# RWKV bonus sums and head layernorm of a hybrid diffusion step: products with constant matrices in two fp32r parts instead of one fp32 product

## The chip, the cores and the metric

The kernel runs on one core of one Trainium2 chip. Its time is the device time of one execution in microseconds (us); of a kernel the median of its runs counts. Five engines work beside each other, each through its own list of instructions in order: TensorE (PE, with PEld for its weight loads), VectorE (DVE), ScalarE (ACT), GpSimd (POOL) and SyncE (SP), which issues most of the transfers. TensorE writes into banks of PSUM, from which ACT or DVE take results.

## The reference, cut to what matters

Two layers of a diffusion trunk over 128 context and 256 latent tokens (T = 384 columns side by side), width 1024. The first layer's mixer holds a Mamba-2 group and an RWKV-7 group; the second holds GLA and mLSTM. The change touches the last lines of the RWKV group (16 heads of 64 channels):

```python
def head_layernorm(x, w, b, n_heads):
    xf = x.reshape(shp[:-1] + (n_heads, shp[-1] // n_heads)).astype(jnp.float32)
    mu = jnp.mean(xf, axis=-1, keepdims=True)
    var = jnp.mean(jnp.square(xf - mu), axis=-1, keepdims=True)
    y = ((xf - mu) * lax.rsqrt(var + RWKV_LN_EPS)).reshape(shp).astype(x.dtype)
    return y * w + b
...
y_rw = head_layernorm((ys_rw[0] + ys_rw[1]).reshape(bsz, t, D_RWKV), p['rwkv_ln_w'], p['rwkv_ln_b'], RWKV_HEADS)
bonus = jnp.sum(rh * kh * p['rwkv_r_k'], axis=-1, keepdims=True) * vh
y_rw = (y_rw + bonus.reshape(bsz, t, D_RWKV)) * g
out = jnp.concatenate([y_ssd, y_rw], axis=-1) @ p['w_out']
```

## The kernel before

Channels lie on the 128 partitions and tokens along the free axis, so an RWKV tile j (0 to 7) is two heads by 384 tokens. A mean or a sum over the 64 channels of a head is then a product with a constant 128x128 matrix: `blk` (ones within a head) gives a head's sum on each of its partitions, and `cen` (identity less 1/64 within a head) takes the mean away. Three such products are made for each j, 24 in all, each one fp32 matmul of 128x384:

- in `rw_bonus` (line 1169): `pb = blk @ rk`, with rk = r * r_k * k in a tile whose name is `t` in the trace; then `bo = v * pb` on DVE;
- in `rw_tail` (line 1451): `pm = cen @ y`; ACT squares it into a tile `t` and copies it back to y; then a second product `blk @ sq`, which the trace also calls `pm<-t`; ACT makes 1/sqrt from it (Ln, Exp), DVE multiplies, adds the bonus and multiplies with the gate product `pg`.

A fourth product of this kind, `pn` (the norm of kk in `rw_shared`), is not touched. The large products (`dps`, projections and MLP) are already made in parts: weights and activations are split in a high part of type fp32r (an ACT copy, line 277) and a low part (a DVE subtraction, line 235), and a product is three fp32r matmuls, high by high, high by low and low by high.

The mixer of the first layer fills the stretch from about 60 to 860 us. `ab_streams` (line 1527) goes through 19 rounds. In a round several generators run interleaved: `tail` (j of two rounds ago), `chain` (the recurrence), `inv` (inverses of 64x64 triangles in f16), `prep` with the bonus at its end, `ssd` (Mamba), and `fill` (dense projections, the modulation product `mod`, at the end the output projection). `run` (line 1584) calls the generator that is furthest behind, and a table of paces weights them. The instructions are so written in one sequence; when the program is built, each engine's list is then put in an order by estimates of when operands and buffers are ready, so that what is written side by side can stand apart. On the chip each engine keeps to its list: an instruction that waits holds up all behind it.

Buffers that matter here: `psP` has two PSUM banks, shared in turn by `pb`, `pm`, `pn`, `pw`, `pa`, `pst`, `pg` and the pairs of `psc`. The pool `misc` has the tags `nh` (two buffers: the neighbour sums `nb` of the token shift) and `nt` (two buffers: the gate temporaries `sg`, and `yr`, the tiles of the mixer's output that `reload` (line 1904) brings back from HBM). In round 16 `ab_norm` (line 1855) reloads eight such tiles through the two `nt` buffers, scales each on DVE and splits it (`sH` on ACT, `sL` on DVE) for the output projection. In round 18 the tail of j = 7 ends the mixer; its y is split and multiplied with `wlast` in `ab_out_last` (line 1937), with the modulation products `mod` of the second layer in between.

Of the kernel before, what the change touches and what calls it, by code (L numbers as in the profile page):

```python
# [8 lines left out]
F32 = mybir.dt.float32  # L9
F32R = mybir.dt.float32r  # L10
# [4 lines left out]
ALU = mybir.AluOpType  # L15
# [6 lines left out]
T = 384  # L22
# [153 lines left out]
class Net:  # L176
# [903 lines left out]
    def rw_evac(self, idx, make, act=True):  # L1080
# [14 lines left out]
            self.stt(out[:, 128:T], nb[:, 129:385], self.mu_h[:, idx:idx + 1], out[:, 128:T], ALU.mult, ALU.add)  # L1095
        return evac

    def rw_low(self):

        self.sigmoid(self.wdt, self.wdt, scale=2.0)  # L1100
        self.ts(self.wdt, self.wdt, 2.0, ALU.mult, -1.0, ALU.add)
# [67 lines left out]
    def rw_bonus(self, j, sh):  # L1169
        rk = self.rpp.tile([128, T], F32, tag="t1", name="t1", bufs=1)  # L1170
        self.stt(rk, sh["r"], self.par("rwkv_r_k", j), sh["k"], ALU.mult, ALU.mult)
        yield
        pb = self.psp("pb")
        self.mm(pb[:, :T], self.c("blk"), rk)
        sh["bo"] = bo = self.rpc.tile([128, T], F32, tag="bo", name="bo", bufs=2)
        self.tt(bo, sh["v"], pb[:, :T], ALU.mult)
        yield
# [273 lines left out]
    def rw_tail(self, j, sh, y):  # L1451

        nc = self.nc
        tl = lambda nm, shape, bufs=1, dt=F32: self.rpc.tile(shape, dt, tag=nm, name=nm, bufs=bufs)
        g2 = tl("g2", [128, 128])
        nc.sync.dma_start(out=g2, in_=self.I["rwkv_g2"][0, :, 128 * j:128 * j + 128])
        pm = self.psp("pm")[:, :T]
        self.mm(pm, self.c("cen"), y)
        sq = tl("t3", [128, T], 1)
        self.act(sq, pm, AF.Square)  # L1460
        self.acopy(y, pm)
        yield
        pm2 = self.psp("pm2")
        self.mm(pm2[:, :T], self.c("blk"), sq)
        rs = tl("t3", [128, T], 1)
        self.act(rs, pm2[:, :T], AF.Ln, bias=self.c("bias")[:, 2:3], scale=1.0 / 64)
        self.act(rs, rs, AF.Exp, scale=-0.5)
        self.tt(y, y, rs, ALU.mult)
        self.stt(y, y, self.par("rwkv_ln_w", j), sh["bo"], ALU.mult, ALU.add)
        yield  # L1470
        pg = self.psp("pg")
        self.mm(pg[:, :T], g2, self.gdt)
        self.stt(y, y, self.par("rwkv_ln_b", j), pg[:, :T], ALU.add, ALU.mult)
        self.dump("y_rw%d" % j, y)
        if j < 7:
            nc.sync.dma_start(out=self.yd[8 + j], in_=y)
        yield
# [480 lines left out]
    def mixer_ab(self):  # L1958
# [90 lines left out]
        for nm in ("AO0", "AO1", "Zb", "AHb", "ALb"):  # L2049
            t = self.rpi.tile([128, 6, 128], F16, name=nm)  # L2050
            self.nc.gpsimd.memset(t, 0.0)
            bd.append(t)
        self.AOb, (self.Zb, self.AHb, self.ALb) = bd[:2], bd[2:]
        self.rpp = self.pool("rwp", es=eb)
        self.yss = self.sumsq()
# [524 lines left out]
```

## Time and profile before

| what | value |
|---|---|
| time, median of 3 runs (lowest to highest) | 1855.35 us (1853.92 to 1860.46) |
| the profiled execution: its own time | 1853.32 us |
| its span on the core, mean granted TensorE clock | 1851.2 us, 0.98 |
| PE busy, PEld busy | 95%, 80% of the span |
| DVE, ACT, POOL busy | 70%, 58%, 12% |
| chain that ended last, by engine | PE 75%, DVE 10%, ACT 8%, DMA 4% |

Matmuls are pipelined, so the busy time of PE counts the way of a matmul through the array as well as the time in which it keeps the next one out; a matmul of 128x384 in fp32r shows some 345 ns, while a row of them starts every 170 to 180 ns. The chain is followed back from the last instruction: at each step to what released it, or to the instruction before it on its engine; the pieces are in us, and time on the chain is what the end was waiting for.

### The profile page before, as it was taken

The numbers are of one execution on the slowest core, as the hardware profiler recorded it, in microseconds if no ns is written. First come the engines' busy times: TensorE is split into PE (matmuls) and PEld (weight loads), VectorE is DVE, ScalarE is ACT, GpSimd is POOL, SyncE is SP. The second block draws the span as 40 slices with busy tenths as digits, with TensorE's granted clock in tenths as the row PEclk, the third lists the DMA queues.
The fourth block names the chain that finished last, engine by engine and source line by source line (L and its number), as shares of the span: only waits on it lengthen the run. The fifth ranks groups of instructions, "written<-read, shape, count | busy, mean of one in ns | idle before, by whom it ended". The sixth has DMA issues, their size and how long they took to land.

```text
span 1851.2 us, 37384 instructions
## 1 busy us (share of the span) xinstructions
PE 1765.5 (95%) x13661; PEld 1480.9 (80%) x13661; DVE 1301.8 (70%) x2992; ACT 1069.6 (58%) x2688; POOL 216.6 (12%) x270
## 2 busy tenths in 40 slices
PE   7879999999999999999999999899999998999998
PEld 3667767766666677786999998889989897999887
DVE  3698788777878889758766334786786958766434
ACT  3567475746574777646655333777676756755322
POOL 3222111110112011101000000020211212000000
PEclk9889999999999999999999999999999998999999
DMA  8332443333334322345445643333333233344432
GB/s 280 112 88 65 123 133 97 106 87 112 102 105 126 101 65 81 100 119 175 117 124 171 177 146 101 102 91 102 102 94 92 74 108 106 115 125 126 150 134 80
DMA packets 314107, 213.55 MB, mean 115 GB/s; under 512 B 39648, under 2 KB 297494, under 8 KB 313924
## 3 DMA queue, kind: packets, MB, share of 16 engines
q1 hardware_dynamic: 308756, 208.35, 38.6%
q10 hardware_dynamic: 4816, 2.69, 0.5%
q8 instruction: 107, 1.75, 0.4%
q14 instruction: 76, 0.62, 0.1%
q0 software_dynamic: 352, 0.13, 0.0%
HBM read 201.32 MB, written 9.78 MB: 114 GB/s over the span
## 4 chain that ended last, share of the span: by engine, by line
PE 75%; DVE 10%; ACT 8%; DMA 4%; issue 2%; POOL 1%; SPq 0%; DVEq 0%; ACTq 0%; POOLq 0%
PE dps L221 45%; PE o L221 7%; PE ps L221 4%; PE mod L221 3%; PE aux L221 2%; DVE wL L235 2%; PE psc L221 2%; DMA raw<-in_w_mod 2%; PE py L221 1%; PE pt L221 1%; DVE cacc L242 1%; PE pr L221 1%; ACT wH L277 1%; PE pw L221 1%; ACT Zb L277 1%
## 5 line engine op out<-in xcount | busy, mean ns | idle before, releaser
L277 ACT ACTIVATE wH<-raw 128x256 fp32r<-128x256 f32 (+1 forms) x790 | 363.3, 480 | 429.3 <-PE dps L221 309.6
L235 DVE TENSOR_TENSOR wL<-raw,wH 128x256 fp32r<-128x256 f32 (+2 forms) x771 | 398.9, 536 | 243.2 <-ACT wH L277 239.5
L277 ACT ACTIVATE Zb<-pz 64x384 f16<-64x384 f32 x160 | 77.2, 483 | 36.4 <-PE pz L221 34.1
L242 DVE SCALAR_TENSOR_TENSOR cacc<-rows,params,cacc 128x384 f32<-128x384 f32 (+1 forms) x192 | 94.2, 491 | 0.7
L221 PE MATMUL dps<-sH,wH 128*128 128x384 f32 x232 | 85.8, 371 | 4.0 <-DVE m L235 3.5
L221 PE MATMUL dps<-sL,wH 128*128 128x384 f32 x232 | 80.5, 347 | 0.3 <-DVE sL L235 0.2
L221 PE MATMUL dps<-sH,wL 128*128 128x384 f32 x232 | 79.7, 345 | 0.5 <-DVE wL L235 0.5
L221 PE MATMUL dps<-h0H,wH 128*128 128x384 f32 (+1 forms) x147 | 58.9, 401 | 8.2 <-ACT h0H L277 3.5
L235 DVE TENSOR_TENSOR AO<-AHb,rwmask 128x768 f16<-128x768 f16 (+1 forms) x112 | 60.1, 537 | 7.7 <-PE pz L221 6.0
L235 POOL TENSOR_TENSOR BK<-BK,kkk 128x768 f32<-128x768 f32 x16 | 33.8, 2110 | 221.5 <-DVE BK L239 150.5
L221 PE MATMUL mod<-xT,cond 128*32 128x384 f32 (+1 forms) x320 | 55.2, 485 | 3.8 <-DVE Q L235 2.5
L221 PE MATMUL dps<-h6H,wH 128*128 128x384 f32 (+2 forms) x147 | 54.9, 373 | 2.7 <-ACT wH L277 2.7
L221 PE MATMUL dps<-h2H,wH 128*128 128x384 f32 (+1 forms) x147 | 55.6, 378 | 1.4 <-ACT wH L277 1.4
L221 PE MATMUL dps<-h4H,wH 128*128 128x384 f32 (+1 forms) x147 | 54.9, 378 | 2.1 <-ACT h4H L245 2.1
L235 POOL TENSOR_TENSOR gDb<-gb 128x384 f32<-128x384 f32 x28 | 33.2, 1187 | 173.5 <-DVE gb L2230 73.2
L221 PE MATMUL dps<-h1H,wH 128*128 128x384 f32 (+1 forms) x147 | 52.0, 354 | 0.0
L221 PE MATMUL dps<-h6H,wL 128*128 128x384 f32 (+2 forms) x147 | 50.8, 346 | 1.2 <-DVE wL L235 1.2
L221 PE MATMUL dps<-h0H,wL 128*128 128x384 f32 (+1 forms) x147 | 51.7, 351 | 0.0
L221 PE MATMUL dps<-h1H,wL 128*128 128x384 f32 (+1 forms) x147 | 51.6, 351 | 0.0
L221 PE MATMUL dps<-h0L,wH 128*128 128x384 f32 (+1 forms) x147 | 51.5, 356 | 0.0
L221 PE MATMUL dps<-h1L,wH 128*128 128x384 f32 (+1 forms) x147 | 51.3, 355 | 0.0
L221 PE MATMUL dps<-h2H,wL 128*128 128x384 f32 (+1 forms) x147 | 51.1, 348 | 0.0
(1163 smaller groups left out, 5450.0 us busy)
## 6 DMA issues: line engine op xcount, KB each, us to landing
raw<-in_w_mlp_up SPq DMA_DIRECT2D x64, 512.0 KB
raw<-in_w_mlp_down SPq DMA_DIRECT2D x64, 512.0 KB
raw<-in_w_in_ab SPq DMA_DIRECT2D x204, 128.0 KB
xT<-in_w_mod SPq DMA_DIRECT2D x128, 192.0 KB
raw<-in_w_in_cd SPq DMA_DIRECT2D x192, 128.0 KB
raw<-in_w_mod SPq DMA_DIRECT2D x64, 192.0 KB
raw<-in_w_mod SPq DMA_DIRECT2D x32, 256.0 KB
raw<-in_w_out_cd SPq DMA_DIRECT2D x64, 128.0 KB
```

The lines of the kernel that those rows point to most:

```text
L221: self.nc.tensor.matmul(out, lhsT, rhs, start=start, stop=stop)
L235: return (eng or self.nc.vector).tensor_tensor(out=out, in0=a, in1=b, op=op)
L242: self.nc.vector.scalar_tensor_tensor(out=out, in0=a, scalar=s, in1=b, op0=op0, op1=op1)
L277: self.nc.scalar.activation(out=out, in_=in_, func=AF.Copy)
```

## The change

A helper `mm_parts` makes a product with a constant matrix in two fp32r matmuls that add up in one PSUM bank: a high part of the operand (`xH`, copied to fp32r on ACT, in an `nh` buffer) and the rest (`xL`, subtracted on DVE, in an `nt` buffer). The three products above go through it. The constants are copied to fp32r once (`blkr`, `cenr`, two DVE copies while the mixer is set up). `blk` has only ones and zeros, `cen` only multiples of 1/64.

```diff
--- before.py
+++ after.py
@@ -1095,6 +1095,15 @@
             self.stt(out[:, 128:T], nb[:, 129:385], self.mu_h[:, idx:idx + 1], out[:, 128:T], ALU.mult, ALU.add)
         return evac
 
+    def mm_parts(self, out, lhsT, x):
+
+        h = self.mpool.tile([128, T], F32R, tag="nh", name="xH", bufs=2)
+        lo = self.mpool.tile([128, T], F32R, tag="nt", name="xL", bufs=2)
+        self.acopy(h, x)
+        self.tt(lo, x, h.bitcast(F32), ALU.subtract)
+        self.mm(out, lhsT, h, stop=False)
+        self.mm(out, lhsT, lo, start=False)
+
     def rw_low(self):
 
         self.sigmoid(self.wdt, self.wdt, scale=2.0)
@@ -1171,7 +1180,7 @@
         self.stt(rk, sh["r"], self.par("rwkv_r_k", j), sh["k"], ALU.mult, ALU.mult)
         yield
         pb = self.psp("pb")
-        self.mm(pb[:, :T], self.c("blk"), rk)
+        self.mm_parts(pb[:, :T], self.blkr, rk)
         sh["bo"] = bo = self.rpc.tile([128, T], F32, tag="bo", name="bo", bufs=2)
         self.tt(bo, sh["v"], pb[:, :T], ALU.mult)
         yield
@@ -1455,13 +1464,13 @@
         g2 = tl("g2", [128, 128])
         nc.sync.dma_start(out=g2, in_=self.I["rwkv_g2"][0, :, 128 * j:128 * j + 128])
         pm = self.psp("pm")[:, :T]
-        self.mm(pm, self.c("cen"), y)
+        self.mm_parts(pm, self.cenr, y)
         sq = tl("t3", [128, T], 1)
         self.act(sq, pm, AF.Square)
         self.acopy(y, pm)
         yield
         pm2 = self.psp("pm2")
-        self.mm(pm2[:, :T], self.c("blk"), sq)
+        self.mm_parts(pm2[:, :T], self.blkr, sq)
         rs = tl("t3", [128, T], 1)
         self.act(rs, pm2[:, :T], AF.Ln, bias=self.c("bias")[:, 2:3], scale=1.0 / 64)
         self.act(rs, rs, AF.Exp, scale=-0.5)
@@ -2050,6 +2059,11 @@
             t = self.rpi.tile([128, 6, 128], F16, name=nm)
             self.nc.gpsimd.memset(t, 0.0)
             bd.append(t)
+
+        self.blkr = self.rpi.tile([128, 128], F32R, name="blkr")
+        self.nc.vector.tensor_copy(self.blkr, self.c("blk"))
+        self.cenr = self.rpi.tile([128, 128], F32R, name="cenr")
+        self.nc.vector.tensor_copy(self.cenr, self.c("cen"))
         self.AOb, (self.Zb, self.AHb, self.ALb) = bd[:2], bd[2:]
         self.rpp = self.pool("rwp", es=eb)
         self.yss = self.sumsq()
```

The numbers of matmuls, copies and subtractions are 24 more each on PE, ACT and DVE (an fp32 matmul goes through the array in two passes that the trace shows apart, so the count of passes stays); POOL's list is the same. The order of PE, DVE, ACT and SP moves around each of the 24 places. Three of them follow.

PE, the first bonus product (`pb`, j = 0), before:

```order
L221 MATMUL aux<-vw,bt 128x256
L221 MATMUL pb<-t_1843,const_base 128x384
L221 MATMUL dps<-h0H,wH 128x384
L221 MATMUL dps<-h0L,wH 128x384
L221 MATMUL dps<-h0H,wL 128x384
L221 LDWEIGHTS AO_795
```

and now, with the second part 62 rows behind the first:

```order
L221 MATMUL aux<-vw,bt 128x256
L221 MATMUL pb<-xH,blkr 128x384
L221 MATMUL dps<-h0H,wH 128x384
L221 MATMUL dps<-h0L,wH 128x384
L221 MATMUL dps<-h0H,wL 128x384
L221 MATMUL dps<-h1H,wH 128x384
...
L221 MATMUL pb<-xL,blkr 128x384
```

The bank of `pb` is open from the first part to the second, across other streams' matmuls. Of the 24 pairs ten stand side by side and fourteen apart like this one.

DVE, round 16, where the tiles `yr` come back from HBM through the two `nt` buffers, before:

```order
L242 SCALAR_TENSOR_TENSOR yr<-yr,params,ssq 128x384 x2
L235 TENSOR_TENSOR AO<-AHb,rwmask 64x384
L235 TENSOR_TENSOR sL<-yr,sH 128x384
L235 TENSOR_TENSOR AO<-AHb,rwmask 64x384
L239 TENSOR_SCALAR UV<-pu 64x2x64
L235 TENSOR_TENSOR sL<-yr,sH 128x384
```

and now:

```order
L242 SCALAR_TENSOR_TENSOR yr<-yr,params,ssq 128x384 x2
L239 TENSOR_SCALAR UV<-pu 64x2x64
L235 TENSOR_TENSOR W<-const_base,AO 128x384
L235 TENSOR_TENSOR sL<-yr,sH 128x384 x2
L235 TENSOR_TENSOR xL<-y,xH 128x384
L235 TENSOR_TENSOR Stmp<-S,pd 128x64
```

The low part of the tail of j = 6 (`xL<-y`) takes an `nt` buffer after the first two of the eight `yr`, so that from there the reloads have one turn more to wait for.

PE, the tail of j = 7 in round 18 and what follows it, before:

```order
L221 MATMUL pm_13242<-t_13239,const_base 128x384
L221 MATMUL pg<-gdt,g_13235 128x384
L221 MATMUL mod<-raw,cond 32x384 x9
L221 MATMUL dps<-sH,wlast 128x384 x2
L221 MATMUL mod<-raw,cond 32x384
L221 MATMUL dps<-sL,wlast 128x384
```

and now:

```order
L221 MATMUL pm_13361<-xH,blkr 128x384
L221 MATMUL pg<-gdt,g_13349 128x384
L221 MATMUL mod<-raw,cond 32x384 x4
L221 MATMUL pm_13361<-xL,blkr 128x384
L221 MATMUL mod<-raw,cond 32x384 x9
L221 MATMUL dps<-sH,wlast 128x384 x2
L221 MATMUL dps<-sL,wlast 128x384
```

The `mod` product that stood between the first products with `wlast` now stands ahead of them, and four more of them ahead of the second part. On DVE the same tail had two low parts of weights (`wL`, 128x512) ahead of `y<-y,t` and a third between it and the next row with y; now `xL`, `y<-y,t` and the two further rows with y stand one behind another, and these `wL` come later.

## Rows read from the trace of the kernel before

**Rows 1.** The page, part 1: busy time, share of the span, instructions, by engine

```profile
PE 1765.5 (95%) x13661; PEld 1480.9 (80%) x13661; DVE 1301.8 (70%) x2992; ACT 1069.6 (58%) x2688; POOL 216.6 (12%) x270
```

**Rows 2.** The page, part 4: the chain that ended last, by engine

```profile
PE 75%; DVE 10%; ACT 8%; DMA 4%; issue 2%; POOL 1%; SPq 0%; DVEq 0%; ACTq 0%; POOLq 0%
```

**Rows 3.** Busy time by stretch: the mixer's middle, and a part of it

```profile
core 0: us, PE busy (x) PEld busy (x) DVE busy (x) ACT busy (x) POOL busy (x), PEclk, DMA share, GB/s
150.00:850.00 700.00, 677.11 (x7466) 493.10 (x7467) 555.67 (x1390) 430.19 (x1095) 93.73 (x101) 0.99 0.37 106
...
550.00:750.00 200.00, 194.62 (x2215) 144.22 (x2208) 168.62 (x422) 127.49 (x329) 30.41 (x26) 1.00 0.33 94
```

**Rows 4.** Instructions on pm and pb: duration ns min/median/max, first and last start

```profile
L221 PE MATMUL pm<-y,const_base x16: 483/486/590, 253.5 to 839.9; 128*128 128x384 f32 x16
L221 PE MATMUL pm<-t,const_base x16: 483/486/590, 266.8 to 841.6; 128*128 128x384 f32 x16
...
L221 PE MATMUL pb<-t,const_base x16: 486/486/1009, 150.4 to 765.3; 128*128 128x384 f32 x16
```

**Rows 5.** The chain: start us, us, what; products and a row of dense matmuls

```profile
150.53 0.65 PE pb L221 x2
...
805.86 5.40 PE dps L221 x30
...
839.70 0.66 PE pm L221 x2
```

**Rows 6.** Instructions on yr: the same split of a 128x384 tile

```profile
L277 ACT ACTIVATE sH<-yr x13: 507/524/538, 707.1 to 807.1; 128x384 fp32r<-128x384 f32 x13
L235 DVE TENSOR_TENSOR sL<-yr,sH x13: 540/552/559, 708.1 to 807.7; 128x384 fp32r<-128x384 f32 x13
```

**Rows 7.** DVE in order of time, set-up of the mixer: copies of constants, a wait

```profile
64.19 0.21 DVE L1647 CAST negb<-const_seq 128x128 bf16<-128x128 f32 x1
64.33 0.68 DVE L1044 CAST rwmask<-rwc 128x1024 f16<-128x1024 f32 x1
69.50 0.42 DVE L235 TENSOR_TENSOR wL<-raw,wH 128x256 fp32r<-128x256 f32 x1 [4.50 <-ACT wH L277]
```

**Rows 8.** The chain in round 16: the reloads

```profile
776.39 3.72 DMA yr<-yd
...
781.25 2.29 DMA yr<-yd
...
785.71 3.69 DMA yr<-yd
```

**Rows 9.** The chain in round 18: the tail of j = 7

```profile
834.94 0.62 PE dps L221 x2
...
840.38 0.49 ACT t L245
840.87 0.38 ACT y L277
841.25 1.03 ACT wH L277 x2
...
843.90 0.60 DVE wL L235
...
847.58 1.42 PE mod L221 x2
849.00 1.54 PE dps L221 x4
```

**Rows 10.** Busy time by stretch, end of the tail (columns as in Rows 3)

```profile
844.80:846.70 1.90, 0.00 (x0) 0.00 (x0) 0.85 (x2) 0.52 (x1) 0.00 (x0) 1.00 0.83 264
846.70:850.50 3.80, 3.77 (x10) 1.69 (x11) 1.08 (x2) 0.00 (x0) 0.00 (x0) 0.55 0.91 310
```

**Rows 11.** In order of time, round 18: a bank of pm, and PE's wait for the tail

```profile
839.53 0.81 PE L221 MATMUL pm<-y,const_base 128*128 128x384 f32 x2
...
840.77 0.49 ACT L277 ACTIVATE y<-pm 128x384 f32<-128x384 f32 x1
...
846.73 0.84 PE L221 MATMUL dps<-sH,wlast 128*128 128x384 f32 x2 [1.99 <-ACT sH L277]
```

## The prediction, made before the changed kernel ran

> **What bounds the kernel now.** I read the page first, then the stretch of the first layer's mixer, since all 24 products lie there. Over the whole span PE is busy 95%, DVE 70%, ACT 58% [rows 1], and the chain that ended last runs over PE for 75%, over DVE for 10% and over ACT for 8% of the span [rows 2]. So PE ends most things, but of what DVE does in 1301.8 us some 185 us (10% of 1851.2) were waited for, and of ACT's 1069.6 us some 148 us (8%): about 14% of the work of either. In the mixer, 150 to 850 us, PE is busy 677 of 700 us and DVE 556, ACT 430 [rows 3]. The engines that the change loads are therefore not full, but they are not idle either, and the reader should keep the 14% in mind: work added there costs a seventh of itself if it falls where the present work falls.
>
> **What goes from PE.** An fp32 product shows as two matmul records of 486 ns each [rows 4], but records overlap, so I take what a product holds up on the chain: 0.65 us for the first `pb` and 0.66 us for the last `pm`, while 30 fp32r matmuls of the same 128x384 in a row take 5.40 us, 0.18 us each [rows 5]. Two parts are 0.36 us, so one product gives back 0.30 us where PE is what is waited for. Following the chain through the mixer I count 15 of the 24 products on it (all eight `pb`, seven `pm`; the first and last of them are in [rows 5]), 11.9 us in sum. 15 x 0.30 = 4.5 us less. The bounds: if all 24 counted, 7.2 us; if each pair cost what two fp32r matmuls cost right after a wait, 0.62 us [rows 9], 24 x 0.04 = 1 us.
>
> **What comes to ACT and DVE.** 24 high parts and 24 low parts of 128x384. The trace has the same split of the same shape on the reloaded tiles: 524 ns on ACT, 552 ns on DVE [rows 6]. That is 12.6 us on ACT and 13.2 us on DVE. By the seventh from above 1.8 us and 1.9 us of it end up in the time; the bounds are nothing (all beside PE's work) and all of it, 25.8 us. I take 3.7 us, since these instructions are strewn among the present ones, whose share I know. The two copies of constants at set-up are 0.21 us each by the nearest row, a 128x128 copy to bf16; they stand behind the copy of the mask, after which DVE sits idle for 4.50 us until ACT is ready [rows 7]. Cost: nothing; without that cover 0.4 us.
>
> **What the buffers do.** In round 16 the chain goes through the reloads of the mixer's output: pieces of 3.72, 2.29 and 3.69 us [rows 8], since each pair of tiles waits for the pair before to leave the two `nt` buffers. The changed order puts the low part of the tail of j = 6 into one of these two after the second tile. It holds the buffer for its subtraction (0.55 us) and until PE has read it, and the reload behind it starts that much later: I take 1.0 us. Below, nothing, if the other buffer sets the pace; above, one whole transfer of 3.7 us. The second low part of that tail comes behind all eight reloads on DVE and delays only its own y, which is needed a round later. POOL's `nb` now shares the two `nh` buffers with the high parts; they are read within about a microsecond, and I cost it at nothing, up to 1 us.
>
> **The tail that ends the mixer.** With j = 7 nothing is left to hide behind. The first product waited for PE: y was there before the dense matmuls ahead of it ended, and the two parts (1.08 us) fit into that wait. The second is in the open: after the square (0.49 us at 840.38) the split adds 1.08 us and PE gives 0.30 back, about 0.8 us more; but in the chain before, ACT made two weight copies ahead of the Ln (1.03 us), and DVE one low part of 0.60 us in the middle of y [rows 9], and the changed order has all of these later. So the tail itself comes out at +0.8 - 0.6 - 0.3 (part of the ACT copies), say -0.1 us. Behind it PE sat idle for 1.99 us until ACT had split y [rows 11], and after that idle stretch the granted clock was 0.55 from 846.7 to 850.5 us [rows 10], the half level of 1.2 GHz for most of it; a `mod` product of 1.42 us stood there on the chain, and four matmuls took 1.54 us [rows 9]. In the changed order that `mod` product, and others, fill the idle time ahead. I take 0.4 us for it, between nothing (its weights have not landed) and 2.2 us (the `mod` piece off the chain, and the four matmuls at the full level). Together -0.5 us, bounds -2.2 and +1.1.
>
> **The sum.** -4.5 + 3.7 + 0 + 1.0 - 0.5 = -0.3 us against the profiled execution's 1853.3 us, which lies 2.1 us above its span: 1853.0 us. The median of the runs is 2.0 us above that execution, so I expect 1855.0 us: no change that can be told. About 0.5%, 9.3 us, is what a measurement of this kernel can tell from no change.
>
> **The rivals.**
>
> Only PE counts. If the added ACT and DVE work all lies in idle time (DVE 144 us of 700, ACT 270 [rows 3]), the reloads don't move and each product gives its 0.30 us, the gain is 7.2 us, with the 2.2 us of the tail 9.4 us: 1846 us. For it speaks that PE is busy 97% of the mixer; against it, that 18% of the chain are ACT and DVE [rows 2], and that nine of the products were not on it. Half of this case lies under the bound of 0.5%.
>
> DVE becomes the bound. In 550 to 750 us DVE is busy 168.6 of 200 us, and PE's weight loads 144.2 [rows 3]. If PE's busy time is mostly the way through the array, and DVE is the fuller engine there, then what PE gives back is worth nothing and each low part costs its whole length: 13.2 us, with ACT's 1.8 us 15 us more, 1868 for this execution, 1870 us for the median. It decides from the point where DVE's idle stretches are all waits for a value that DVE itself made a step earlier. Against it: DVE has only 10% of the chain. The Trainium skill ("Perfetto Trace Analysis", Identifying the Most-Contended Engine) says that for the vector engine occupancy is a fair measure of how full it is and for TensorE matmul busy time is not, weight-load time being the better one; by it DVE (79% of 150 to 850 us) stands above PE (70%) and should not be given more. The chain of this trace does not agree, and I give the case the smaller chance.
>
> An open bank holds up the others. Two PSUM banks serve eight kinds of product. Before, the bank of a `pm` was held from 839.53 us to the end of the copy at 841.26 us [rows 11], 1.7 us. Now 14 of 24 pairs stand apart, and their bank is open for at least the subtraction and the wait for DVE's turn, 1.08 us more. If each of these delays the next product by so much on the chain, 15 us come and 4.5 go: 1866 us. It decides where a pair of `psc`, which wants both banks, is next. Against it: other streams' matmuls stand between the parts, so that PE itself goes on, and eight of the fourteen pairs would have to be in the way of a product that is due.
>
> That fp32r parts are no faster than fp32 is excluded by [rows 5].
>
> **How the numbers follow.** The forecast has a chance of 0.58, with its own range 1849 to 1861 us; only PE 0.17; DVE the bound 0.13; the open bank 0.12. Faster by over 0.5%: half and a little of the second, 0.10, and 0.03 from a tail that gains all it can: 0.13. Slower: the DVE case 0.13, half of the open banks 0.06, and 0.03 from an order that falls badly somewhere else: 0.22. Within 0.5%: 0.65. The range that should hold the time 8 times in 10 reaches from the PE case, 1846, to the DVE case less its last microseconds, 1868 us.
>
> **What the profile of the changed kernel would show.** PE term: pieces of `pb` and `pm` on the chain of some 0.36 us for two matmuls, or 0.18 each where they are apart. Split term: 24 `xH` near 524 ns and 24 `xL` near 552 ns, with PE's waits for `xL` short (under 4 us in sum); if they are 10 us and more, the ACT and DVE term is too small. DVE case: PE idle in 550 to 750 us rises by several us. Open bank: `psc`, `pw` or `pn` wait for a reader of `pb` or `pm`. Reloads: the chain between the first and the last `yr` grows by about 1 us. Tail: the clock from the first `wlast` product on, and whether a `mod` piece is still between them. The prediction is wrong if the stretch 150 to 850 us changes by more than some 6 us either way; it would be wrong in its reasons if that stretch is the same but the pieces above are not, or if the time moves after 860 us, where no instruction changed.

## The result

The changed kernel takes 1873.37 us (median of 9 runs, 1864.02 to 1876.6) beside 1853.92 us (9 runs, 1851.59 to 1860.46): a ratio of 1.0095, 95% interval 1.0075 to 1.0115. By the ratio it is slower by about 18 us (the medians lie 19.5 us apart), and outside the range that I gave. Its profiled execution took 1876.6 us, with a span of 1874.5 us at a mean granted clock of 0.971 (before: 0.98).

The page after: busy time by engine, and the chain that ended last by engine.

```profile
PE 1778.1 (95%) x13661; PEld 1491.1 (80%) x13661; DVE 1314.8 (70%) x3018; ACT 1079.6 (58%) x2712; POOL 217.4 (12%) x270
...
PE 78%; DVE 9%; ACT 5%; DMA 3%; issue 3%; POOL 1%; SPq 1%; DVEq 0%; ACTq 0%; POOLq 0%
```

Beside [rows 1, 2]: DVE and ACT are busy 13.0 and 10.0 us more (I had added up 13.2 and 12.6), and their shares of the chain went down. PE's busy time rose by 12.6 us, though every product became shorter. The busy time by stretch after, for the two stretches of [rows 3] (PE, PEld, DVE, ACT, POOL with their counts, then the granted clock):

```profile
150.00:850.00 700.00, 673.79 (x7377) 494.11 (x7375) 554.72 (x1382) 432.09 (x1099) 94.06 (x100) 0.97 0.35 99
550.00:750.00 200.00, 191.74 (x2135) 141.99 (x2135) 166.33 (x412) 126.14 (x324) 28.70 (x25) 0.94 0.32 89
```

The clock was 0.99 and 1.00 there. What PE got done in 550 to 750 us fell from 2215 matmuls to 2135. The pieces themselves are as expected (the split and the parts after, for [rows 4, 6]; the last pair on the chain, for [rows 5]):

```profile
L277 ACT ACTIVATE xH<-t x16: 507/523/544, 148.6 to 858.5; 128x384 fp32r<-128x384 f32 x16
L235 DVE TENSOR_TENSOR xL<-t,xH x16: 540/551/560, 151.1 to 860.3; 128x384 fp32r<-128x384 f32 x16
L221 PE MATMUL pb<-xH,blkr x8: 338/432/477, 149.2 to 784.5; 128*128 128x384 f32 x8
L221 PE MATMUL pb<-xL,blkr x8: 333/420/443, 152.7 to 784.7; 128*128 128x384 f32 x8
```

```profile
857.38 0.34 PE pm L221 x2
```

**Where the time went.** I compared the starts of the same PE instructions in the two traces, as a median for each 25 us; I call the difference the lag. The changed kernel lies 1.3 us ahead until 250 us, 5.1 behind from 275, 16.1 behind from 650, 24.0 behind from 875, and 22.8 at the end. These are three large steps, at or near a tail; between them, and so over most of the 24 products, the lag changes by some 2 us at most. The first step is at 262 to 283 us, around the second product of the tail of j = 0. Two products for the modulation (`mod`) wait there (PE in order of time, with the idle time ahead in brackets):

```profile
268.05 0.81 PE L221 MATMUL mod<-xT,cond 128*32 128x384 f32 x2 [1.09 <-DVE cacc L239]
...
282.63 1.33 PE L221 MATMUL mod<-xT,cond 128*32 128x384 f32 x2 [1.12 <-DMA xT<-in_w_mod]
```

The granted clock was 0.65 from 268 to 272 us and 0.57 from 282.6 to 286.6. In the kernel before the longest wait of a `mod` product there is 0.43 us, and the clock is 1.00 from 262 to 280 us. The loads of these weights stand at other places in SP's list. The second step is near 650 us (PE in the same way, then stretches of both kernels around it):

```profile
641.36 0.35 PE L221 MATMUL pw<-W,Zb 128*128 128x64 f16 x6 [1.07 <-ACT Zb L277]
...
650.97 0.33 PE L221 MATMUL pr<-S,KR 64*64 64x64 f32 x4 [0.94 <-DVE S L235]
...
652.08 1.65 PE L221 MATMUL psc<-KR,BK 64*128 64x128 f32 x6 [0.78 <-DVE BK L235]
```

```profile
640.00:653.00 13.00, 9.86 (x93) 7.38 (x92) 11.42 (x32) 5.97 (x14) 2.45 (x1) 0.94 0.27 80
652.00:676.00 24.00, 23.92 (x219) 18.71 (x220) 16.95 (x45) 12.03 (x28) 3.05 (x3) 0.51 0.16 43
```

The same two stretches of the kernel before, which has no wait of over 0.4 us there:

```profile
636.00:646.00 10.00, 9.59 (x91) 7.30 (x92) 8.85 (x28) 5.28 (x13) 1.81 (x1) 1.00 0.34 100
646.00:670.00 24.00, 23.46 (x330) 18.32 (x327) 23.56 (x60) 16.55 (x41) 5.70 (x4) 1.00 0.26 66
```

None of the waits is for `xH`, `xL`, `pb` or `pm`. Ahead of `S` on DVE stands a row that took 2.18 us (`cacc` at 647.84 us, 0.61 us for the next such row) while a row of POOL ran beside it (2.45 us from 647.16). PE idles for some 3 us, then runs at the half level (1.2 GHz) for 24 us and gets 219 matmuls done instead of 330. The third step is in round 18, after (the chain; DVE; PE):

```profile
862.24 6.00 DMA raw<-in_w_mlp_up
868.23 0.02 issue
868.25 0.64 ACT wH L277
868.89 0.02 issue
868.92 0.69 DVE wL L235
869.61 0.47 DVE m L235
870.08 0.04 issue
870.13 1.33 PE dps L221 x3
871.45 1.42 PE mod L221 x2
```

```profile
868.92 0.69 DVE L235 TENSOR_TENSOR wL<-raw,wH 128x512 fp32r<-128x512 f32 x1 [2.88 <-ACT wH L277]
```

```profile
865.50 0.61 PE L221 MATMUL dps<-sH,wlast 128*128 128x384 f32 x2 [1.24 <-ACT sH L277]
...
870.13 0.69 PE L221 MATMUL dps<-sH,wlast 128*128 128x384 f32 x1 [3.07 <-DVE m L235]
```

Beside [rows 9, 11]: the tail itself came when it should (PE waits 1.24 us for it, 1.99 before). But a `wL` that stood ahead of y now stands between it and the rows `m<-m,dps`. It waits for weights that land at 868.23 us, and the third product with `wlast` waits 3.07 us for `m`.

### The profile page after: what moved, and what is told of

Same layout as the page of the kernel before. It is cut to its first block, busy times and chain, and to the rows that moved or that the text cites. A ratio compares the mean times of both kernels' runs of the same rounds, so it can differ in the third digit from the quotient of the medians.

```text
span 1874.5 us, 37435 instructions
## 1 busy us (share of the span) xinstructions
PE 1778.1 (95%) x13661; PEld 1491.1 (80%) x13661; DVE 1314.8 (70%) x3018; ACT 1079.6 (58%) x2712; POOL 217.4 (12%) x270
## 4 chain that ended last, share of the span: by engine, by line
PE 78%; DVE 9%; ACT 5%; DMA 3%; issue 3%; POOL 1%; SPq 1%; DVEq 0%; ACTq 0%; POOLq 0%
PE dps L221 46%; PE o L221 7%; PE ps L221 5%; PE mod L221 3%; PE aux L221 2%; PE psc L221 2%; DVE wL L235 2%; PE py L221 2%; PE pr L221 1%; PE pt L221 1%; DVE cacc L242 1%; PE pw L221 1%; PE ms L221 1%; PE pu L221 1%; ACT wH L277 1%
## 5 line engine op out<-in xcount | busy, mean ns | idle before, releaser
L221 PEld LDWEIGHTS dps<-sH,wH 128*128 128x128 f32 x232 | 43.7, 189 | 13.0 <-issue 5.8
```

The costliest lines, as they stand in the source:

```text
L221: self.nc.tensor.matmul(out, lhsT, rhs, start=start, stop=stop)
```

## The experiments

Theory A: the time is lost by the order into which the engines' lists fell, and by the granted clock after the waits that this brings. Theory B: by the splits' work on ACT and DVE. Theory C: by the cheaper products, which keep PE less busy. For each kernel I give the ratio to the kernel before, and two sums worked out from all its runs: span times mean granted clock (what the program needs at the full level, waits included) and span times the rest (what the half level cost). The 94 runs of the kernel before that lie beside these have 1812.8 and 38.8 us; the columns are differences from that (a bookkeeping over whole runs, not the price of single waits), and their standard errors are 0.3 to 1.0 us and 0.9 to 3.8 us.

| kernel | ratio (95%) | full-clock part | half-clock part |
|---|---|---|---|
| changed kernel | 1.0095 (1.0075 to 1.0115) | +6.3 | +11.7 |
| e1: bonus alone | 0.9986 (0.9975 to 0.9998) | +0.2 | -2.1 |
| e2: tails alone | 1.0108 (1.0087 to 1.0129) | +5.9 | +15.2 |
| e3: splits unread | 1.0078 (1.0053 to 1.0103) | +6.7 | +8.5 |
| e4: PE's side, 16 products | 1.0057 (1.0041 to 1.0072) | +2.3 | +9.3 |
| e5: old work, new lists | 1.0130 (1.0111 to 1.0148) | +9.1 | +12.5 |
| e6: 12 products, old lists | 1.0056 (1.0036 to 1.0076) | +5.1 | +5.9 |
| e7: the same 12, free lists | 1.0051 (1.0033 to 1.0069) | +0.5 | +9.6 |
| e8: all but tail 7 | 1.0060 (1.0044 to 1.0077) | +2.2 | +9.6 |
| e9: e6 with earlier splits | 1.0029 (1.0013 to 1.0045) | +5.1 | +0.5 |
| e10: changed, idle time filled | 1.0085 (1.0060 to 1.0109) | +8.9 | +7.9 |
| e11: old kernel, other pace | 1.0015 (1.0001 to 1.0029) | +3.1 | -0.5 |
| e12: e9 with splits unread | 1.0034 (1.0015 to 1.0052) | +3.4 | +1.3 |
| e13: e9, tails 1 to 5 | 1.0012 (0.9995 to 1.0028) | +4.5 | -0.9 |
| e14: e9, tail 0 | 1.0000 (0.9983 to 1.0017) | -0.5 | +1.5 |
| e15: all but tails 0 and 7 | 1.0052 (1.0034 to 1.0070) | -1.1 | +11.7 |

### One part of the change at a time

e1 keeps the call in `rw_bonus`, e2 the two in `rw_tail`; e3 and e4 change the helper:

```diff
 e3:
     self.acopy(h, x)
     self.tt(lo, x, h.bitcast(F32), ALU.subtract)
-    self.mm(out, lhsT, h, stop=False)
-    self.mm(out, lhsT, lo, start=False)
+    self.mm(out, lhsT, x)
 e4 (rk and sq written as F32R):
-    self.acopy(h, x)
-    self.tt(lo, x, h.bitcast(F32), ALU.subtract)
-    self.mm(out, lhsT, h, stop=False)
-    self.mm(out, lhsT, lo, start=False)
+    self.mm(out, lhsT, x, stop=False)
+    self.mm(out, lhsT, x, start=False)
```

> Only the eight bonus products are made in two parts; the sixteen of the tail stay fp32. Theory A (the loss comes from the lists' new order at three places, 262-283, 645-663 and 842-865 us, and not from the parts): round 18 has its three wL rows together ahead of the gated y, as in the kernel before, so no step at 842-865 us (-6 against the changed kernel); the step at 262-283 us belongs to the first tail and goes too; 1854 us, between 1850 and 1861, the upper end if the step at 650 us comes back. Theory B (the added ACT and DVE work itself costs, 20 us over 24 splits): 8/24 of it, 1860 to 1861 us, spread evenly. Theory C (fewer PE cycles let the clock fall): about the same as B, with more half-clock stretches than before.

> Only the sixteen products of the tail are made in two parts; the bonus stays fp32. Theory A: round 18 has a wL between the m rows, as in the changed kernel, so the step at 842-865 us is there (+6), that at 262-283 us probably too (+6), that at 650 us open: 1866 us, between 1858 and 1876. Theory B: 16/24 of 20 us, 1867 us, but spread evenly over the eight tails, 1.6 us each. The lag of the same PE instructions behind the kernel before tells them apart: steps under A, a slope under B.

> All 24 splits are made on ACT and DVE in the same buffers, but nothing reads them: the 24 products stay fp32. So all of the added ACT and DVE work (12.6 and 13.2 us) without any change to PE. Theory A: the work itself costs a seventh, 3.7 us; round 18 keeps its wL rows ahead of y, so no step there: 1858 us, between 1852 and 1866 (another order may bring a step of its own). Theory B: all of the loss and the 5 to 7 us that PE no longer gives back: 1878 us or more, as a slope.

> PE's side alone, for 16 of the 24 products (bonus and variance): their operands are written as fp32r where they are made and multiplied twice, so the low part is left out and the sums are doubled; no ACT or DVE work is added; the products that take the mean away stay fp32. Theory A: 16 x 0.30 us at most, -3 to -5 us, 1850 us, unless the order of round 18 (a wL between the m rows here too) brings its +6: then 1856 us with a step at 842-865 us. Theory B: 1849 us, no step. Theory C: slower than before, with new half-clock stretches near the products.

Measured: 1852.11, 1873.15, 1869.54 and 1866.15 us. The whole loss sits with the tails; the bonus alone is a little faster than before. e4 has no split and still loses 0.57%, which speaks against B. A did not have its time either; only C had it slower with more half clock (+9.3 us). But e3 has PE's old products and loses 0.78%, with +8.5 us of half clock, which speaks against C, and is outside A's range as well. What e2, e3 and e4 share with the changed kernel is that the lists around the tails fell anew.

### The lists held

Here the order is taken out of the building program's hands: each engine's list is chained to an order read from another kernel.

```diff
+def pin(tc, nc):
+    ...
+    for e, text in ORDER.items():
+        o = np.cumsum(np.frombuffer(zlib.decompress(base64.b85decode(text)), "<i2").astype(int))
+        for a, b in zip(o, o[1:]):
+            tc.add_manual_dep(by[e][b], by[e][a].name, dep, reason="order")
```

> The work of the kernel before (24 fp32 products, no splits), but PE, DVE, ACT, SP and POOL are held to the order of the changed kernel's lists, with the splits and second parts left out; only the eight bonus products find their own place on PE. Theory A (the order costs, not the parts): 1868 to 1876 us, with the steps of the changed kernel at 262-283 us (+6), 645-663 us (+10, or none of it in executions that keep the clock) and 842-865 us (+6). Theory B (the splits cost) and theory C (the cheaper products let the clock fall): no step, 1854 us.

> The mirror of it: the twelve products of the tails j = 0 to 5 are made in two parts, with their splits on ACT and DVE, but all five engines are held to the order of the kernel before, the splits and second parts put in beside the products. Theory A: no steps, and what PE gives back, 12 x 0.1 to 0.3 us: 1850 to 1854 us, a lag that stays between -4 and +1 us. Theory B: 12/24 of 20 us, 1862 to 1864 us, as a slope over 250 to 700 us. Theory C: half-clock stretches beyond the 17 us that the kernel before has between 150 and 1000 us.

> The same twelve products in two parts as in the held kernel, the same instructions on every engine, but the lists are put in order by the program's own estimates. Theory A: the steps of the kernel with only the tails in parts at 262-300 us (+10) and 600-660 us (+7), none in round 18: 1866 us, between 1860 and 1872. Theory B and C: the same as the held kernel, whatever that is.

e5 took 1875.55 us: the work of the kernel before, without one split, loses in the new lists as much as the changed kernel and more. Holding the lists costs nothing in itself: e14 below, held to the old ones in the same way, has the time of the kernel before. The profiled execution of e5, the fastest of its five, has the wait of `pw`, and in round 18 the late transfer, `wL` and `m` one behind another:

```profile
637.21 0.35 PE L221 MATMUL pw<-W,Zb 128*128 128x64 f16 x6 [1.07 <-ACT Zb L277]
```

```profile
850.67 5.43 DMA raw<-in_w_mlp_up
...
856.12 0.64 ACT wH L277
...
856.78 0.69 DVE wL L235
857.47 0.48 DVE m L235
```

With the same lists, the changed kernel is faster than e5 by 0.35% (0.08 to 0.62%, 1.0095 against 1.0130): in the lists made for them the parts are a gain, some 6 us with wide bounds (1.5 to 11.5).

The mirror, e6 (1863.19 us), did not come back to the time before: A's number for it failed, and B's (1862 to 1864 us) was met. I suspected my own hand: I had put both halves of a split 20 matmuls ahead of the product, and DVE waited 10.1 us in sum for the high parts. e7, with the same instructions in free lists, has the same time (1863.28 us), as B said and within A's range too, but made up in another way: 0.5 us at the full clock, 9.6 us of half clock.

> The same twelve products of the tails j = 0 to 5 in two parts, all five engines again held to the order of the kernel before, but the splits are put in at better places: the high part on ACT some 40 matmuls ahead of the product, the low part on DVE some 16 ahead (both stood 20 ahead, and DVE waited 10.1 us in sum for the high parts). Theory A with this correction (the loss of the held kernel came from where I had put the splits): DVE's waits for xH under 3 us in sum, PE's for xL under 1 us, no step of over 2 us at 262-300 us, 1851 to 1856 us. Theory D (splits in the tail cost PE time wherever they stand): 1861 to 1865 us again.

> The twelve splits of the tails j = 0 to 5 stand on ACT and DVE at the same places as in the held kernel with early splits, but nobody reads them: PE's list is word for word that of the kernel before, with fp32 products. PE alone differs between the two held kernels. If the 0.29% of the held kernel with early splits is PE waiting for the parts: this one is no slower than before, 1852 to 1855 us. If it is the time of 6.1 us on ACT and 6.6 us on DVE in lists that had no room: 1858 to 1861 us, and slower than the kernel with the parts by what the parts give back, 1 to 3 us. Theory A in its plain form (work beside PE costs nothing) expects the first.

e9 (1860.2 us) has 0.29% instead of 0.56%, above A's range and just under D's; DVE's waits for `xH` are 2.1 us, but PE's for `xL` 2.6 us still. What went is half clock; at the full clock both have +5.1 us, so the better places gained nothing there. e12 (1859.3 us), whose PE list is that of the kernel before, loses the same, and A in its plain form (work beside PE costs nothing) fails here. So twelve splits in lists that had no room for them cost 0.3%, whether PE reads them or not, and no gain of the parts is seen between the two (-0.05%, give or take 0.25).

In one execution each, both show their lag at 262 to 300 us. ACT has no gap of over 0.2 us there until 272 us, so I suspected that place:

> As the held kernel with early splits, but without the first tail: the ten products of the tails j = 1 to 5 in parts, five lists held as before. If its 0.3% came from the one place at 262 to 300 us (a high part put into a gapless stretch of ACT that PE waits for, and the half clock behind it): 1849 to 1853 us, a ratio of 0.997 to 1.000 with no step. If each split costs its share (a seventh, or half of its time): 10/12 of 0.3%, 1858 us.

> The other part: only the two products of the first tail (j = 0) in parts, five lists held as before. If it is the place: all of it, +0.3%, 1857 to 1860 us, with a half-clock stretch near 290 us in most executions. If it is the number of splits: 2/12 of it, 1854 to 1855 us.

e13 took 1857.61 and e14 1853.87 us beside 1854.76: the place was wrong. The profiled e14 does have the stretch of half clock there, and its lag rises to 8.3 us, but it falls back to 4.0 at 425 us and 0.3 at 850, where the kernel before has half clock in its turn; over twelve runs nothing is left. At the full clock the cost goes with the splits of tails 1 to 5 (+4.5 us for ten), though e13's whole time can't be told from that of the kernel before.

### Single places of the changed kernel

> The changed kernel, but the two products of the last tail (j = 7) stay fp32; 22 of 24 in parts. The lists are those of the changed kernel up to round 18; there the wL rows stand ahead of y again and not between the m rows. Theory A: the step at 842-865 us is gone, -6: 1867 us by the median, with the lag the same as that of the changed kernel up to 840 us. Theory B: -2/24 of 20 us, 1871 to 1872 us.

> The changed kernel with its free order, but the first and the last tail (j = 0 and 7) stay fp32: 20 of 24 products in parts. At 262 us the loads of w_mod stand in SP's list as in the kernel before, and in round 18 the wL rows stand ahead of y. Places, not numbers: the steps at 262-283 and 842-865 us are gone, 1852 to 1860 us (the upper end if the order near 650 us still costs). Numbers: 20/24 of the loss, 1869 us.

```diff
-        self.mm_parts(pm, self.cenr, y)
+        (self.mm_parts(pm, self.cenr, y) if 0 < j < 7 else self.mm(pm, self.c("cen"), y))
```

(and so for `pm2`; e8 has `j < 7`.) e8 took 1865.03 us: 0.35% less than the changed kernel, 4.1 us of it at the full clock, and the step in round 18 is gone. That settles this place: the reorder there cost what it seemed to. e15 took 1863.4 us, between its two expectations; the step at 262 us is gone too, and at the full clock it is 1.1 us ahead of the kernel before. But 11.7 us of half clock remain. Its profiled execution shows two places (PE; stretches ahead of and behind each):

```profile
593.64 1.29 PE L221 MATMUL mod<-xT,cond 128*32 128x384 f32 x8 [1.51 <-DVE Q L235]
...
640.14 0.35 PE L221 MATMUL pw<-W,Zb 128*128 128x64 f16 x6 [1.07 <-ACT Zb L277]
```

```profile
590.00:594.00 4.00, 2.49 (x36) 1.76 (x39) 3.85 (x8) 2.24 (x7) 1.29 (x1) 0.99 0.13 33
594.00:604.00 10.00, 10.00 (x55) 4.96 (x47) 6.09 (x19) 0.83 (x2) 0.87 (x1) 0.50 0.37 118
636.00:641.00 5.00, 3.72 (x60) 2.41 (x57) 5.00 (x15) 2.76 (x9) 0.00 (x0) 1.00 0.49 128
641.00:649.00 8.00, 7.90 (x38) 6.11 (x38) 5.41 (x15) 2.36 (x8) 2.06 (x1) 0.57 0.29 83
```

The kernel before at the first of these places:

```profile
593.27 0.85 PE L221 MATMUL mod<-xT,cond 128*32 128x384 f32 x8 [0.61 <-DVE Q L235]
```

```profile
590.00:594.00 4.00, 3.39 (x44) 2.21 (x43) 3.75 (x10) 2.71 (x9) 1.66 (x1) 1.00 0.22 61
594.00:604.00 10.00, 9.92 (x71) 4.96 (x67) 6.84 (x19) 2.25 (x6) 0.87 (x1) 1.00 0.64 194
```

The same instruction waits 1.51 us instead of 0.61, the clock behind it is 0.50 instead of 1.00, and 55 matmuls start in ten microseconds instead of 71. The longer wait does not come from the lists: those of DVE and POOL are the same around it in both kernels. What differs is which of two rows started first. In e15 a row of POOL started 0.20 us ahead of a row of DVE (`cacc`), and the latter took 1.51 us; in the kernel before it started 0.09 us behind it, and `cacc` took 0.62 us, POOL's row 1.66 instead of 1.29. `Q`, for which `mod` waits, comes next on DVE. e15, then the kernel before:

```profile
591.61 1.51 DVE L242 SCALAR_TENSOR_TENSOR cacc<-rows,params,cacc 128x384 f32<-128x384 f32 x1
591.41 1.29 POOL L235 TENSOR_TENSOR E<-E 128x512 f32<-128x512 f32 x1 [2.74 <-ACT E L245]
```

```profile
592.13 0.62 DVE L242 SCALAR_TENSOR_TENSOR cacc<-rows,params,cacc 128x384 f32<-128x384 f32 x1
592.22 1.66 POOL L235 TENSOR_TENSOR E<-E 128x512 f32<-128x512 f32 x1 [3.06 <-ACT E L245]
```

Of the 17 profiled executions here, this `mod` waits 1.50 to 1.52 us in twelve and 0.61 or 0.62 us in five; a stretch of half clock follows in seven of the twelve and in none of the five. That one row held up the other is read from the traces, not tested. And the place does not settle where e15's loss comes from, for e1 has the same pair and is not slower (PE; the stretch behind it):

```profile
589.92 1.40 PE L221 MATMUL mod<-xT,cond 128*32 128x384 f32 x8 [1.50 <-DVE Q L235]
```

```profile
590.00:600.00 10.00, 10.00 (x54) 5.03 (x55) 6.37 (x19) 0.83 (x2) 0.87 (x1) 0.50 0.35 108
```

The second place has the wait of `pw` that the changed kernel shows at 641.36 us.

> The changed kernel with its lists held as they are, and 16 more products of 128x384 on PE (into a bank that nobody reads) ahead of the third pair with wlast in round 18, where PE sat idle for 3.07 us and the granted clock then was 0.50 for 6.8 us. If the half clock comes from the idle stretch: PE waits under 1 us there, the clock of the stretch behind stays at 1.00, and the step at 842-865 us shrinks from 6.3 to some 3 to 4 us. If the clock falls whatever PE does there (or by the kind of product): 0.50 again at the same place, and the step grows by the products' own time, if at all.

```diff
+            if j == 2:
+                p = self.psp("fill")
+                for _ in range(16):
+                    self.mm(p[:, :T], h[:, cs], xh)
             ps = self.dacc()[:, :T]
```

e10 took 1869.99 us. PE at this place, then the stretches of e10 and, below, those of the changed kernel:

```profile
864.52 2.99 PE L221 MATMUL fill<-sH,wlast 128*128 128x384 f32 x16
868.16 0.45 PE L221 MATMUL dps<-sH,wlast 128*128 128x384 f32 x1 [0.66 <-DVE m L235]
```

```profile
866.00:870.00 4.00, 3.35 (x16) 2.15 (x15) 2.69 (x5) 3.53 (x8) 0.10 (x1) 1.00 0.99 347
870.00:874.00 4.00, 4.00 (x22) 2.99 (x21) 3.34 (x5) 2.66 (x7) 2.88 (x3) 1.00 0.95 320
874.00:878.00 4.00, 3.71 (x25) 2.58 (x25) 4.00 (x7) 2.62 (x7) 2.26 (x2) 1.00 0.36 138
```

```profile
866.00:870.00 4.00, 1.06 (x5) 0.65 (x4) 1.12 (x4) 1.54 (x3) 0.00 (x0) 0.99 1.03 379
870.00:874.00 4.00, 3.87 (x9) 2.20 (x10) 1.69 (x4) 4.00 (x11) 1.97 (x2) 0.50 1.00 348
874.00:878.00 4.00, 4.00 (x15) 2.86 (x13) 2.61 (x5) 0.62 (x2) 1.00 (x1) 0.66 0.89 320
```

With products in the idle time the clock stays at 1.00 and the step shrinks from 6.3 to 3.6 us, as expected of the idle stretch as cause; PE still waits 0.66 us for `m` behind them. The whole kernel's ratio does not tell this apart from the changed kernel's.

> The kernel before with one number changed in the table of paces: the tail's generator counts as 1.15 times as long, so that its lines are written a little later among the others. All products fp32, no split, the same instructions; some 560 rows of PE's list differ, about as many as under the change (625). Theory A (whatever touches the tails throws the order anew, and the order before is a good one): slower than before by 3 to 20 us, with steps at the tails. Theory B, C, D: the time of the kernel before, 1854 us within 3 us.

```diff
-PACE = {"cdo0": 1.034, ...
+PACE = {"tail": 1.15, "cdo0": 1.034, ...
```

e11 took 1856.44 us, +0.15%: at most a little slower, 2.7 us where A had 3 to 20, and within the 3 us of the other theories. A new order need not cost much; it is these orders that do.

## Why the prediction was wrong

**The step that failed** is one that the sum did not have: the price of the new order of the lists away from the edited products. I costed the moved order only where an edit stands, put it at nothing elsewhere, and gave "an order that falls badly somewhere else" 3 chances in 100. e5 shows that the new lists alone, with the old work, cost 1.30% (1.11 to 1.48), more than the whole change. Two thirds of the change's loss (11.7 of 18 us) is half clock, which I had thought of only at the end of the tail. In the kernels whose free lists moved around the tails (e2, e3, e4, e7, e8, e15) this part is +8.5 to +15.2 us, whatever stands on PE; in four of the five held to the old lists it is -0.9 to +1.5 (e6: +5.9). It need not be so: e11's free lists moved as well, and it has -0.5.

**The tail of j = 7**, -0.5 us: the lag there grew by 6.3 us. I read "these `wL` come later" as a gain, since they left the way of y. I did not ask what they would stand in front of, nor when their weights land. The `mod` piece of [rows 9] was still there, 1.42 us at 871.45. e8 confirms place and size.

**ACT and DVE**, +3.7 us for 24 splits: the durations were right, the seventh was not. Twelve splits in the old lists cost 6.3 us (e12: 0.34%, 0.15 to 0.52) where the term has 1.9; so B was right in part. My own sign for this, waits of PE for `xL` of 10 us and more, did not show: in the changed kernel they are 1.3 us in sum. The eight bonus products gave back at least what their splits cost (e1). A share of the chain, taken over a long stretch, says little of work put into particular places.

**PE**, -4.5 us: the size of a pair was right (0.34 us on the chain, 0.36 expected). That it pays in full is not shown: e9 against e12 has no gain, while the changed kernel against e5 has 6 us, 2.8 of them at the full clock.

**Reloads** [rows 8], +1.0 us: between 775 and 800 us the lag grows by 1.8 us. But it grows by the same 1.8 us in e5, where no `xL` takes a buffer; so this too goes with the order, and the buffer's turn is not shown to cost anything. **Constants** [rows 7], 0: no lag before 250 us.

**The rivals.** DVE did not become the bound: in 550 to 750 us it was busy 166.3 us, 168.6 before. PE's idle time there did rise, from 5.4 to 8.3 us, which was my sign for this case, but the old work in the new lists (e5) loses as well. No `psc`, `pw` or `pn` waited for a reader of `pb` or `pm`. My own mark, 6 us in 150 to 850 us, was passed by far (17.7 at 825 us).

**What stays open.** Why the clock falls behind one wait and not another like it: the changed kernel's profiled execution has the 1.51 us wait of `mod` as well, at 598.91 us, and no half clock behind it. So that the half clock goes with these orders is shown by the runs, but which waits bring it in the median is not. And what order would suit all 24 parts: only e1 beats the kernel before, by 0.14%.

## What to carry to other kernels

Where a program puts the lists in order, a small edit is two changes, the work and the order; hold the lists as they were (or give the old work the new lists) before crediting either. Read the new order away from the edit too: for each instruction that moved, ask what now stands behind it and when its own operand lands. And a new wait of PE can cost more than its length: in e15 0.9 us more of waiting was followed by ten microseconds at half clock. How often that happens takes several runs to tell, since e1 shows the same in its profiled execution and is no slower.

## What I had not expected of the hardware

One program spreads widely with the clock: e5's five runs go from 1864.72 us at a mean granted clock of 0.980 to 1883.62 us at 0.968, with the same lists. So the lag in one profiled execution shows where time can be lost, not what is lost in the median: e14 lost 6.7 us at one place and gave it back at two others.
